# A sparse 3x3 convolution: the first 32 rows of the input are loaded by two transfers instead of one

## The chip, the core and the metric

The kernel runs on one core of one Trainium2 chip. The metric is device time in microseconds (us). Below, PE is the matrix engine, PEld its weight loads, DVE the vector engine, ACT the scalar engine, POOL the GpSimd engine and SP the engine that here only issues transfers. A core has 16 DMA engines that every transfer is spread over.

## The reference

`x` is 16 images of 64 channels of 64x64, float32. `weight` is 128x64x3x3, float32, nine tenths of it zero; the kernel treats it as dense.

```python
x_pad = np.pad(x, ((0, 0), (0, 0), (pad, pad), (pad, pad)), mode='constant')
output = np.zeros((batch, c_out, h, w), dtype=np.float32)
for b in range(batch):
    for co in range(c_out):
        for ci in range(c_in):
            for kh in range(k):
                for kw in range(k):
                    if weight[co, ci, kh, kw] != 0:
                        output[b, co] += weight[co, ci, kh, kw] * x_pad[b, ci, kh:kh+h, kw:kw+w]
```

The input is 16.8 MB and the output 33.6 MB, both float32.

## The kernel before

**Tiling.** Two images of 64 channels fill the 128 partitions, so there are eight pairs, `xs[0]` to `xs[7]`, each a bf16 tile of 128 x 64 x 64 (rows x columns). Image 0 of a pair sits in the lower 64 partitions, image 1 in the upper 64, and every product is a pair of matmuls, one on each half of the PE array (`64*128` in the profile).

**Loads.** Nearly all of the input comes in through POOL's transfer queue, which converts float32 to bf16 on the way (`load`, L68, and L63 for rows 32 to 63 of the first pair). The first 32 rows of the first pair come another way: SP loads them unconverted as float32 into `x_head` (L62), a tile of the output pool, right after the weights (L60), and DVE and ACT convert them (`cast_x`, L101): rows 0 to 8 on DVE (L123), rows 9 to 17 on ACT (L130), rows 18 to 31 on ACT (L133). POOL issues L63, then the loads of pairs 1 to 3 and of 24 rows of pair 4 at once; the remaining loads follow in `load` calls at the ends of later pairs.

**Weights.** The weights are cast to bf16, transposed on PE against an identity matrix (`transposed`, L111), and copied to `wT` as three row taps G0, G1, G2, with the differences G0-G1 and G2-G1 beside them (`difference`, L115). Around this PE runs matmuls on a zero tile that go nowhere (`keep_busy`, L86): seven before the transposes and seven after.

**Work.** Each pair is cut into four blocks of 16 rows. The first block of the first pair is `direct`: two times 8 rows, each nine taps on both images, 36 matmuls in all, copied out by ACT (L163) and DVE (L164). It needs rows 0 to 16 of the input. Every other block is `twos`: POOL adds neighbouring rows (`s`, L169), PE multiplies the sums once by G1 (6 matmuls), ACT copies the result to SBUF (`pc`, L176), and PE multiplies even and odd rows by the other taps (24 matmuls), whose results DVE adds to `pc` (L183). The second block of the first pair (rows 16 to 31) is the first `twos`; its `s` needs all rows that the second ACT conversion (L133) writes.

**Order.** The schedule is manual: each engine runs its instructions in the order in which the code issues them. On PE that is seven idle matmuls, the transposes, seven idle matmuls, the direct block, then the `twos` blocks. SP issues the weights, the head, the two stores of each pair as the pair ends (L209, half-pair stores for the last pair, L206), and after pair 1 four loads of one word each into a spare tile (L216). The transfers on SP take their completion semaphores in turn from a set of eight.

Of the kernel before, what the change touches and what calls it, by code (L numbers as in the profile page):

```python
# [27 lines left out]
def kernel(  # L28
# [6 lines left out]
    nc = tc.nc  # L35
# [2 lines left out]
    C_OUT, _, KH, KW = weight.shape  # L38
    assert (B, C_IN, H, W) == (16, 64, 64, 64) and (C_OUT, KH, KW) == (128, 3, 3)
    NP = B // 2  # L40
    HEAD = 32

    const_pool = ctx.enter_context(tc.tile_pool(name="const", bufs=1))
    x_pool = ctx.enter_context(tc.tile_pool(name="x", bufs=1))
# [10 lines left out]
    def pair(p):  # L55
        return x[2 * p : 2 * p + 2].rearrange("n i h w -> (n i) h w")
# [2 lines left out]
    w_sb = const_pool.tile([C_OUT, C_IN * KH * KW], FP32, name="w_sb")  # L59
    nc.sync.dma_start(out=w_sb, in_=weight.rearrange("o i kh kw -> o (i kh kw)"))  # L60
    x_head = o_pool.tile([128, H, W], FP32, name="o")
    nc.sync.dma_start(out=x_head[:, 0:HEAD, :], in_=pair(0)[:, 0:HEAD, :])  # L62
    nc.gpsimd.dma_start(out=xs[0][:, HEAD:H, :], in_=pair(0)[:, HEAD:H, :])  # L63
    ident = const_pool.tile([128, 128], BF16, name="ident")
    make_identity(nc, ident)

    def load(p, a=0, b=H):
        nc.gpsimd.dma_start(out=xs[p][:, a:b, :], in_=pair(p)[:, a:b, :])  # L68
# [15 lines left out]
    def keep_busy(n):  # L84
        for _ in range(n):
            nc.tensor.matmul(idle_ps, idle_rhs[:, 0:128], idle_rhs, start=True, stop=True)  # L86
# [13 lines left out]
    def cast_x(copy, a, b):  # L100
        copy(out=xs[0][:, a:b, :], in_=x_head[:, a:b, :])  # L101
# [12 lines left out]
    def difference(g, wps):  # L114
        nc.vector.tensor_tensor(out=wT[:, g], in0=wps, in1=wT[:, G1], op=SUB)  # L115
# [11 lines left out]
    ps2 = transposed(G2)  # L127
    nc.scalar.copy(out=wT[:, G2], in_=ps2)
    keep_busy(7)
    cast_x(nc.scalar.copy, 9, 18)  # L130
    difference(G01, ps0)
    difference(G21, ps2)
    cast_x(nc.scalar.copy, 18, HEAD)  # L133


    def product(terms, rows):
# [22 lines left out]
    def direct(p, o, r0, rows):  # L159
        ps = product(  # L160
            [(xs[p], G1, r0, 1), (xs[p], G0, r0 - 1, 1), (xs[p], G2, r0 + 1, 1)], rows
        )
        nc.scalar.copy(out=o[0][:, r0 : r0 + rows, :], in_=ps[0])  # L163
        nc.vector.tensor_copy(out=o[1][:, r0 : r0 + rows, :], in_=ps[1])  # L164

    def twos(p, o, r0):
        t0 = r0 // 2
        s = s_pool.tile([128, 8, W], BF16, name="s")
        nc.gpsimd.tensor_tensor(  # L169
            out=s, in0=xs[p][:, r0 : r0 + 16 : 2, :], in1=xs[p][:, r0 + 1 : r0 + 16 : 2, :], op=ADD  # L170
        )
        shared = product([(s, G1, 0, 1)], 8)
        pc = []
        for n in range(2):
            c = p_pool.tile([128, 8, W], FP32, name="pc")
            nc.scalar.copy(out=c, in_=shared[n])  # L176
            pc.append(c)
        even = [(xs[p], G21, r0 + 1, 2), (xs[p], G0, r0 - 1, 2)]
        odd = [(xs[p], G01, r0, 2), (xs[p], G2, r0 + 2, 2)]
        for first, terms in ((r0, even), (r0 + 1, odd)):  # L180
            ps = product(terms, 8)
            for n in range(2):
                nc.vector.tensor_tensor(  # L183
                    out=o[n][:, first : r0 + 16 : 2, :], in0=ps[n], in1=pc[n], op=ADD
                )

    for p in range(NP):
        o = [o_pool.tile([C_OUT, H, W], FP32, name="o") for _ in range(2)]
        last = p == NP - 1
        for blk in range(4):  # L190
            r0 = 16 * blk
            if BLOCKS[p][blk] == "T":
                twos(p, o, r0)


                if p == 1 and blk == 3:
                    load(EARLY, CUT, H)
                elif blk == 3 and p in LATER:
                    load(*LATER[p])
            else:  # L200
                for r, rows in ((r0, 8), (r0 + 8, 8)):
                    direct(p, o, r, rows)
            if last and blk % 2 == 1:
                for n in range(2):
                    rows = slice(r0 - 16, r0 + 16)
                    nc.sync.dma_start(out=out[2 * p + n][:, rows, :], in_=o[n][:, rows, :])  # L206
        if not last:
            for n in range(2):
                nc.sync.dma_start(out=out[2 * p + n], in_=o[n])  # L209
        if p == 1:  # L210

            spare = const_pool.tile([1, 4], FP32, name="spare")
            for k in range(4):
                nc.sync.dma_start(out=spare[:, k : k + 1], in_=weight[0:1, 0, 0, 0:1])  # L216


# [28 lines left out]
```

## Time and profile before

| what | value |
|---|---|
| median of 3 runs | 126.06 us (125.97 to 126.77) |
| the profiled execution: span from the first to the last instruction | 127.2 us |
| PE busy | 111.3 us (87%) |
| DVE busy | 82.4 us (65%) |
| POOL, ACT busy | 41.7 us, 38.9 us |
| moved by DMA | 42.91 MB in the queues' count, HBM read 17.07 MB, written 33.55 MB |
| mean granted PE clock | 0.955 |

The profiled execution has one time, its span: 127.2 us, 1.1 us above the median of the timed runs. Bytes in the queues are counted on the side that is written, so a converting load of 4 KB in bf16 reads 8 KB. The share of the 16 DMA engines that is busy stands beside the engines' busy times in the profile's rows of windows; it may exceed 1 in a short window, because a packet is counted where it starts.

### The profile page before, as it was taken

Reading aid. Unit: us, or ns where it says so; the run is one execution under the profiler, and the core shown is the slowest. Engines: PE = TensorE matmul, PEld = TensorE weight load, DVE = VectorE, ACT = ScalarE, POOL = GpSimd, SP = SyncE. Lnnn points to the kernel's source line nnn. Section 1 sums busy time; section 2 is a strip of 40 time slices with the busy share of each in tenths; the row PEclk is TensorE's granted clock in tenths of the full one; section 3 lists DMA queues with packets and bytes.
Section 4 is the critical chain, followed back from the end, with each engine's and each line's share of the span. In section 5 each row is a group of like instructions: output and inputs, shape, how many; then the busy total and the mean of one; then the engine's idle time right before and its main releaser. Section 6 shows DMA issues by size and latency. Waiting matters only on the chain.

```text
span 127.2 us, 2468 instructions
## 1 busy us (share of the span) xinstructions
PE 111.3 (87%) x989; PEld 57.9 (46%) x989; DVE 82.4 (65%) x135; ACT 38.9 (31%) x71; POOL 41.7 (33%) x47
## 2 busy tenths in 40 slices
PE   6939999999999999999999999999999999991000
PEld 2414455555555555555555555555555555550000
DVE  0305357787778777877787778777877787775000
ACT  4504343333333333333333333333333333330000
POOL 6405433353335333533353335333333330000000
PEclk9995999999999999999999999999999999999755
DMA  4999999659999999999999999999999999999991
GB/s 131 346 228 214 222 222 206 137 247 412 299 323 397 419 281 299 330 428 330 296 322 430 353 345 420 413 374 345 421 417 412 433 433 438 412 422 415 435 410 77
DMA packets 4339, 42.91 MB, mean 337 GB/s; under 512 B 488, under 2 KB 488, under 8 KB 1256
## 3 DMA queue, kind: packets, MB, share of 16 engines
q1 hardware_dynamic: 2888, 34.90, 66.0%
q0 software_dynamic: 1440, 7.86, 30.0%
q8 instruction: 7, 0.11, 0.3%
q14 instruction: 4, 0.03, 0.1%
HBM read 17.07 MB, written 33.55 MB: 398 GB/s over the span
## 4 chain that ended last, share of the span: by engine, by line
PE 82%; DMA 6%; DVE 1%; issue 1%; DVEq 0%; SPq 0%
PE ps L150 82%; DMA o<-in_x_dram 6%; DVE o L183 1%; DVEq L242 0%; DVE x L101 0%; SPq L60 0%; DVEq L183 0%
## 5 line engine op out<-in xcount | busy, mean ns | idle before, releaser
L150 PE MATMUL ps<-x,wT 64*128 64x504 bf16 (+3 forms) x780 | 90.5, 379 | 2.3 <-DVE x L101 2.3
L183 DVE TENSOR_TENSOR o<-ps,pc 128x512 f32<-128x512 f32 x124 | 77.8, 685 | 22.1 <-PE ps L150 19.8
L150 PEld LDWEIGHTS <-wT 64*128 64x128 bf16 x966 | 55.3, 95 | 52.0 <-issue 4.7
L169 POOL TENSOR_TENSOR s<-x 128x512 bf16<-128x512 bf16 x31 | 35.6, 1151 | 61.2 <-PE ps L150 42.7
L176 ACT COPY pc<-ps 128x512 f32<-128x512 f32 x62 | 33.3, 589 | 64.0 <-issue 61.8
L150 PE MATMUL ps<-s,wT 64*128 64x512 bf16 (+1 forms) x186 | 25.7, 377 | 0.0
L86 PE MATMUL ps<-idle_rhs 128*128 128x512 bf16 x14 | 5.5, 562 | 1.2 <-DVE idle_rhs L81 1.2
L68 POOL DMA_DIRECT2D x<-in_x_dram x9 | 5.0, 560 | 0.0
L164 DVE COPY o<-ps 128x512 f32<-128x512 f32 x2 | 1.4, 692 | 3.7 <-PE ps L150 3.7
L101 DVE CAST x<-o 128x576 bf16<-128x576 f32 x1 | 0.5, 460 | 4.6 <-DMA o<-in_x_dram 4.6
L86 PEld LDWEIGHTS <-idle_rhs 128*128 128x128 bf16 x14 | 1.8, 136 | 3.6 <-issue 2.2
L105 DVE CAST w_bf<-w_sb 128x192 bf16<-128x192 f32 (+1 forms) x4 | 1.1, 357 | 2.4 <-DMA w_sb<-in_weight_dram 2.4
L101 ACT CAST x<-o 128x576 bf16<-128x576 f32 (+1 forms) x2 | 1.5, 802 | 3.5 <-DMA o<-in_x_dram 3.5
L163 ACT COPY o<-ps 128x512 f32<-128x512 f32 x2 | 1.2, 585 | 4.1 <-PE ps L150 4.1
L105 ACT ACT_TABLE_LOAD x1 | 1.3, 1283 | 0.7 <-PEq L231 0.7
L105 ACT CAST w_bf<-w_sb 128x64 bf16<-128x64 f32 (+1 forms) x2 | 0.7, 416 | 1.6 <-DMA w_sb<-in_weight_dram 1.6
L111 PE MATMUL ps<-ident,w_bf 128*128 128x128 bf16 x9 | 1.2, 309 | 0.0
L111 PEld LDWEIGHTS <-w_bf 128*128 128x128 bf16 x9 | 0.8, 130 | 0.8 <-DVE w_bf L105 0.7
L115 DVE TENSOR_TENSOR wT<-ps,wT 128x384 bf16<-128x384 f32 x2 | 1.0, 547 | 0.0
L63 POOL DMA_DIRECT2D x<-in_x_dram x1 | 0.7, 693 | 0.8 <-POOLq L231 0.8
L81 DVE MEMSET idle_rhs<- 128x256 uint32 x1 | 0.3, 272 | 0.9 <-PEq L231 0.9
L124 ACT CAST wT<-ps 128x384 bf16<-128x384 f32 x1 | 0.5, 478 | 0.4 <-PE ps L111 0.4
(8 smaller groups left out, 1.9 us busy)
## 6 DMA issues: line engine op xcount, KB each, us to landing
out_dram<-o SPq DMA_DIRECT2D x14, 2048.0 KB, 15.1
x<-in_x_dram POOLq DMA_DIRECT2D x5, 1024.0 KB, 15.9
out_dram<-o SPq DMA_DIRECT2D x4, 1024.0 KB, 10.8
x<-in_x_dram POOLq DMA_DIRECT2D x3, 512.0 KB, 13.3
o<-in_x_dram SPq DMA_DIRECT2D x1, 1024.0 KB
x<-in_x_dram POOLq DMA_DIRECT2D x1, 640.0 KB, 15.4
x<-in_x_dram POOLq DMA_DIRECT2D x1, 384.0 KB, 21.9
w_sb<-in_weight_dram SPq DMA_DIRECT2D x1, 288.0 KB
```

The lines of the kernel that those rows point to most:

```text
L68: nc.gpsimd.dma_start(out=xs[p][:, a:b, :], in_=pair(p)[:, a:b, :])
L86: nc.tensor.matmul(idle_ps, idle_rhs[:, 0:128], idle_rhs, start=True, stop=True)
L101: copy(out=xs[0][:, a:b, :], in_=x_head[:, a:b, :])
L105: copy(out=w_bf4[:, g, a:b, :], in_=w_v[:, k : k + b - a, :])
L111: nc.tensor.matmul(wps[:, j, :], src, ident, start=True, stop=True)
L115: nc.vector.tensor_tensor(out=wT[:, g], in0=wps, in1=wT[:, G1], op=SUB)
L150: nc.tensor.matmul(ps[n][:, lo:hi, c_lo:c_hi], tap(g, kw, n), src[q, a:b:step, c_lo + kw - 1 : c_hi + kw - 1], start=(i == 0), stop=(i == ...
L163: nc.scalar.copy(out=o[0][:, r0 : r0 + rows, :], in_=ps[0])
L164: nc.vector.tensor_copy(out=o[1][:, r0 : r0 + rows, :], in_=ps[1])
L169: nc.gpsimd.tensor_tensor(out=s, in0=xs[p][:, r0 : r0 + 16 : 2, :], in1=xs[p][:, r0 + 1 : r0 + 16 : 2, :], op=ADD)
L176: nc.scalar.copy(out=c, in_=shared[n])
L183: nc.vector.tensor_tensor(out=o[n][:, first : r0 + 16 : 2, :], in0=ps[n], in1=pc[n], op=ADD)
```

## The change

The transfer of rows 0 to 31 becomes two transfers on the same queue, of rows 0 to 17 and of rows 18 to 31, issued one after the other. Both have a completion semaphore of their own, so the conversions of rows 0 to 8 (DVE) and 9 to 17 (ACT) wait for the first transfer only and the conversion of rows 18 to 31 (ACT) for the second. One of the four one-word loads after pair 1 goes, so that the number of transfers on SP is the same from there on. The order of instructions on PE, DVE, ACT and POOL is the same.

```diff
-    HEAD = 32
+    FIRST, HEAD = 18, 32
...
     x_head = o_pool.tile([128, H, W], FP32, name="o")
-    nc.sync.dma_start(out=x_head[:, 0:HEAD, :], in_=pair(0)[:, 0:HEAD, :])
+    for a, b in ((0, FIRST), (FIRST, HEAD)):
+        nc.sync.dma_start(out=x_head[:, a:b, :], in_=pair(0)[:, a:b, :])
     nc.gpsimd.dma_start(out=xs[0][:, HEAD:H, :], in_=pair(0)[:, HEAD:H, :])
...
-    cast_x(nc.scalar.copy, 9, 18)
+    cast_x(nc.scalar.copy, 9, FIRST)
     difference(G01, ps0)
     difference(G21, ps2)
-    cast_x(nc.scalar.copy, 18, HEAD)
+    cast_x(nc.scalar.copy, FIRST, HEAD)
...
             spare = const_pool.tile([1, 4], FP32, name="spare")
-            for k in range(4):
+            for k in range(3):
                 nc.sync.dma_start(out=spare[:, k : k + 1], in_=weight[0:1, 0, 0, 0:1])
```

## The prediction

> **What bounds the kernel now.** I read the chain of waits first.
>
> ```profile
> 1.18 8.12 DMA o<-in_x_dram
> 9.30 0.02 issue
> 9.33 0.47 DVE x L101
> 9.80 0.04 issue
> 9.84 103.77 PE ps L150 x954
> ```
>
> PE starts real work at 9.84, when the head has landed (9.30) and DVE has converted nine rows, and then never stops. The timeline shows what lies around that start.
>
> ```profile
> 5.15 2.35 PE L86 MATMUL ps<-idle_rhs 128*128 128x512 bf16 x7
> ...
> 9.33 0.46 DVE L101 CAST x<-o 128x576 bf16<-128x576 f32 x1 [4.61 <-DMA o<-in_x_dram]
> 9.33 1.51 ACT L101 CAST x<-o 128x576 bf16<-128x576 f32 x2 [3.46 <-DMA o<-in_x_dram]
> ...
> 9.84 5.67 PE L150 MATMUL ps<-x,wT 64*128 64x512 bf16 x36 [2.34 <-DVE x L101]
> ...
> 10.92 3.37 POOL L169 TENSOR_TENSOR s<-x 128x512 bf16<-128x512 bf16 x3 [6.31 <-ACT x L101]
> ...
> 15.33 0.83 PE L150 MATMUL ps<-s,wT 64*128 64x512 bf16 x6
> 15.98 2.77 PE L150 MATMUL ps<-x,wT 64*128 64x512 bf16 x24
> ```
>
> The idle matmuls keep PE until 7.50, so a head that is there before that gains nothing more. PE idles 2.34 us, and the direct block's 36 matmuls take 5.67 us, where 24 later ones take 2.77 (36 would take 4.15): 1.5 us go to a granted clock of 0.50 in the window 10 to 12. So the late head costs PE 2.34 + 1.5 = 3.8 us.
>
> Does the end follow PE? PE's last matmul starts at 114.5 and DVE's last add at 115.5, but the span ends at 127.2: the last 11 us are stores draining. The windows by microsecond tell the rest (the width, busy time of PE, PEld, DVE, ACT, POOL with counts, then granted clock, share of the DMA engines, GB/s).
>
> ```profile
> 23.00:24.00 1.00, 1.00 (x14) 0.49 (x11) 0.30 (x1) 0.79 (x2) 0.96 (x1) 1.00 1.02 202
> 24.00:25.00 1.00, 1.00 (x14) 0.57 (x12) 0.97 (x2) 0.00 (x0) 0.00 (x0) 1.00 0.49 92
> 25.00:26.00 1.00, 1.00 (x12) 0.55 (x10) 1.00 (x3) 0.13 (x1) 0.03 (x1) 1.00 0.05 9
> 26.00:27.00 1.00, 1.00 (x14) 0.57 (x10) 0.51 (x1) 0.94 (x2) 1.00 (x1) 1.00 0.62 262
> ```
>
> The DMA engines are full from 2 us until 124.5 except here, between the last early load and the first store (issued at 26.0). The kernel is bound by its transfers; PE's start matters only through this hole. The trace's packet records give it for each engine: fourteen idle 2.1 to 2.7 us, two only 1.2 and 1.4, because their loads end later. An earlier PE therefore gains at least 1.2 us (those two) and at most about 2.3 (the mean of the others), however early it is.
>
> **Why the head is late.** It lands when the last of 16 engines is done. By the semaphore records, fifteen engines report between 5.69 and 6.62; one reports at 9.30. On the fifteen, the eight 8192 B packets (309 ns each) run back to back and POOL's loads begin after the eighth (seventh on two of them). On the late engine POOL's first packet came in at 3.92, after one head packet, and from then on one head packet and one load packet take turns (head packets at 5.84, 6.46, 7.09, 7.71, 8.33). The same taking of turns, one for one whatever the sizes, is in steady state: at 33 to 40 us stores of 16384 B (611 ns) and loads of 5120 B (398 ns) alternate with a period of 1.0 us.
>
> So everything hangs on whether an ordinary execution has that engine. With it gone, PE would start at 7.5, the hole would close, and the span would be 127.2 minus 1.2 to 2.3, thus 124.9 to 126.0. The timed runs' median, 126.06, lies 1.1 below this span. I take that as the likelier reading (about 0.55): most timed runs have no such late engine, and the profiled one does.
>
> **The change part by part.**
>
> *Packets.* 2304 B take 93 ns and 8192 B 309, so 0.0367 ns per byte between: 4608 B take 178 and 3584 B 140. Eight of each are 1.42 + 1.12 = 2.54 us on an engine, against 8 x 0.309 = 2.47: +0.07 us of work, nothing at 122 us of it. SP's extra issue is 0.42 us (L62's own row), behind which SP has nothing until 26.0.
>
> *First transfer, ordinary engines.* Their head data starts at about 2.9 to 3.2, so the first transfer is through at 4.3 to 4.6 and lands, 0.4 later (5.30 to 5.69 in the records), at 4.7 to 5.3 if the semaphore waits one turn. DVE converts until 5.8, ACT its nine rows until 6.0, and DVE's copy to `wT` (0.55) ends by 6.4. PE is still in its idle matmuls until 7.50. Against a head that lands at 6.62 (converted by 7.1) this gains nothing: 7.50 either way.
>
> *Second transfer, ordinary engines.* Loads came in after the eighth packet of the queue, so the second transfer's eight packets probably take turns with L63's eight of 4096 B (322 ns): 8 x (0.322 + 0.140) = 3.7, from 4.6 to 8.3, plus one turn for the semaphore and the 0.4: 9.0. If they do not take turns it is 6.1. ACT's conversion (0.93, the longer of its two) ends at 9.9, POOL's `s` (1.15) at 11.1. PE wants it at 7.50 + 4.15 = 11.65. Cover: 0.5 us, and behind it the hole, 1.2 to 2.3 us, as stores would be ready at about 22.2 while loads run to 24.5. I cost it at nothing; without either cover each microsecond costs one.
>
> *The wait it adds.* ACT's conversion of rows 18 to 31 now waits for a transfer of its own; queued behind it on ACT are the copies of the direct block (L163) and every `pc`, and on POOL every `s`.
>
> *The spare load.* Its four rows stand at 39.9 to 43.3 on SP at 1.0 to 1.3 us each; the next store is issued at 51.6. One fewer: nothing. The semaphores of the first four stores shift by one place; each previous user has landed long before its reuse.
>
> The Trainium skill, "DMA: Bandwidth & Descriptors", section "Rules for kernel authors", speaks against splitting: at least 1 MiB per transfer, and the section on one transfer's anatomy gives about 2.0 us fixed for each. By an estimate from that, the second half would land 2.0 us after 6.62, at 8.6; the rows give 6.1 to 9.0, and both are early enough.
>
> *Sum:* 0 on PE's start, +0.07 on the DMA engines: 126.06 becomes **126.1**, its own range 125.5 to 126.9.
>
> **The rivals.**
>
> *Slower: the second transfer starves on the late engine.* Suppose that engine is in every run. Its first transfer then takes turns with L63: from 3.92 some six or seven packets at 0.322 + 0.178 = 0.5, through at about 7.3, landed at 8.0 (9.30 before). But now eight more packets are to take turns, and L63 is nearly used up: its successor's packets are 8192 B at 0.625 us. Two turns of 0.46 and six of 0.765 are 5.5; with semaphore turns (0.3 and 0.6) and the 0.4 it lands at about 14.0 to 14.5 instead of 9.30. Conversion 0.93 and `s` 1.15 end at 16.1 to 16.6; `s` is wanted at 15.33 today. PE has run dry by then, so another half-speed stretch (1.5, today's price) is possible. Cost 0.8 to 2.9 us, price 1.9: 128.0. It decides from the point where the second transfer lands after 13.2 (15.33 - 1.15 - 0.93), or, where PE starts at 7.5, after 9.5 plus the hole's cover. For it: the turns are in the trace. Against it: one engine of sixteen, seen once. 0.33.
>
> The skill's same page, "Latency and other measured facts", says that DMA engines 7 and 15 are usually slower in traces. The packet records here do not number the engines, so no row shows it. If the late engine is one of them, it is late in every run and this rival's 128.0 stands; by the trace alone it may be chance.
>
> *Faster: the late engine is in every run before, and the shorter first transfer gets past it.* If the first 8 packets of 178 ns are fetched before POOL's descriptors are there and the second lands by 13, PE starts at 7.5 to 8.5 at full clock, 2.8 to 3.8 us earlier; the hole caps it at 1.2 to 2.3: 123.8 to 124.9, say 124.4. For it: the wait is the head of the chain. Against it: the median lies below the span already. 0.20.
>
> *It does not do what it says:* both halves land together, since the loads stay out until sixteen packets are through. Then nothing changes; this is in the forecast's 0.47.
>
> **Numbers.** No change 0.47 (126.1), slower 0.33 (126.9 to 129.0), faster 0.20 (123.8 to 124.9). About 1%, 1.26 us, is what a measurement of this kernel can tell from no change, so the bounds are 124.8 and 127.3. The range leaves out half of the faster case and the top of the slower one: 124.3 to 128.6.
>
> **What would show it.** Right: the DVE conversion waits until about 5, PE's direct block starts at 7.5 without half clock, `s` of the second block is done before 11.7, and the DMA share has no hole at 24 to 26. The slower rival: ACT's second L101 row starts at 13 or later, PE's `ps<-s` row at 12 to 16 waits for POOL or ACT, and the clock halves again. The faster one: PE as in the first case, with runs clearly under 125. I am wrong if the timed runs of before have the late engine after all, or if taking turns hits the second transfer harder than the 0.5 us of cover and the hole can bear.

## The result

The changed kernel is slower. Its median is 128.34 us (127.09 to 130.18, 6 runs), beside 126.11 us (125.97 to 126.77) for the kernel before in the same comparison; the ratio is 1.0123, 95% interval 1.0084 to 1.0161, or 1.5 us (1.1 to 2.0). Some executions of both kernels take 1.5 us or more longer than the rest, for reasons that no trace here shows; ratios and intervals leave them out, which is why this one is below the quotient of the medians.

The profiled execution after has a span of 125.3 us and a time of 127.09: about 1.8 us lie around the span, in most runs of the study 1.7 to 2.0. So the profile that was shown of before, with its span of 127.2, was not that of an ordinary run at 126.1. An ordinary one came with the first experiment, span 124.2, and it is the one to compare with.

The chain of waits after (start, us, what):

```profile
1.64 9.75 DMA o<-in_x_dram
11.39 0.02 issue
11.41 0.95 ACT x L102
12.36 0.07 issue
12.44 1.16 POOL s L170
13.59 0.04 issue
13.63 98.28 PE ps L151 x918
```

It no longer runs through the first rows. It runs through the second transfer: landed at 11.39, converted by ACT, added by POOL, and only then PE's 918 remaining matmuls, without a stop to the end. The timeline of the same execution shows what PE did meanwhile.

```profile
5.24 1.67 PE L87 MATMUL ps<-idle_rhs 128*128 128x512 bf16 x7
...
5.88 0.46 DVE L102 CAST x<-o 128x576 bf16<-128x576 f32 x1 [0.98 <-DMA o<-in_x_dram]
...
6.84 3.98 PE L151 MATMUL ps<-x,wT 64*128 64x512 bf16 x36
...
11.41 0.94 ACT L102 CAST x<-o 128x896 bf16<-128x896 f32 x1 [4.86 <-DMA o<-in_x_dram]
...
12.44 4.48 POOL L170 TENSOR_TENSOR s<-x 128x512 bf16<-128x512 bf16 x4 [7.83 <-ACT x L102]
13.63 0.82 PE L151 MATMUL ps<-s,wT 64*128 64x512 bf16 x6 [2.81 <-POOL s L170]
```

The first transfer does what it says: landed at 5.86, and PE starts the direct block as soon as its idle matmuls end. It finishes at 10.82 and waits 2.81 us. The hole in the transfers at 24 to 26 us, of which the prediction made so much, is hardly there (last columns: granted clock, share of the DMA engines, GB/s).

```profile
23.00:24.00 1.00, 1.00 (x14) 0.55 (x11) 1.00 (x3) 0.00 (x0) 0.00 (x0) 1.00 0.87 172
24.00:25.00 1.00, 1.00 (x14) 0.54 (x12) 0.81 (x2) 0.83 (x2) 0.73 (x1) 1.00 1.04 206
25.00:26.00 1.00, 1.00 (x12) 0.53 (x10) 0.59 (x1) 0.24 (x1) 0.93 (x2) 1.00 1.26 455
```

### The profile page after: what moved, and what is told of

It is laid out like the page before. It is cut to its first block, busy times and chain, and to the rows that moved or that the text cites. A ratio compares the mean times of both kernels' runs of the same rounds, so it can differ in the third digit from the quotient of the medians.

```text
span 125.3 us, 2468 instructions
## 1 busy us (share of the span) xinstructions
PE 109.1 (87%) x989; PEld 57.1 (46%) x989; DVE 82.5 (66%) x135; ACT 38.8 (31%) x71; POOL 41.6 (33%) x47
## 4 chain that ended last, share of the span: by engine, by line
PE 78%; DMA 8%; DVE 1%; POOL 1%; ACT 1%; issue 1%; SPq 1%; DVEq 0%
PE ps L151 78%; DMA o<-in_x_dram 8%; DVE o L184 1%; POOL s L170 1%; ACT x L102 1%; DVEq L243 0%; SPq L63 0%; SPq L60 0%; DVEq L184 0%
## 5 line engine op out<-in xcount | busy, mean ns | idle before, releaser
L151 PE MATMUL ps<-x,wT 64*128 64x504 bf16 (+3 forms) x780 | 88.8, 373 | 0.0
L87 PE MATMUL ps<-idle_rhs 128*128 128x512 bf16 x14 | 4.8, 505 | 1.2 <-DVE idle_rhs L82 1.2
```

The source lines that it names most:

```text
L151: nc.tensor.matmul(ps[n][:, lo:hi, c_lo:c_hi], tap(g, kw, n), src[q, a:b:step, c_lo + kw - 1 : c_hi + kw - 1], start=(i == 0), stop=(i == ...
```

## The experiments

Each ratio is against the kernel before, run beside it on the same chip.

**One transfer, once more** (no edit).

> The kernel before once more, for its span in an ordinary execution; the profile at hand has a span of 127.2 us with one DMA engine reporting the head at 9.30. If that engine is an exception (the reading of the prediction), the profile shows the head landed by 6.7, PE's direct block at about 7.0 to 7.5, the first store issued at about 22 and a span near 124.5 to 125. If it is the rule, PE starts again at 9.8 and the span is again 127.

126.28 us, ratio 0.9985 (0.9955 to 1.0016), span 124.2. Its timeline:

```profile
5.11 2.38 PE L86 MATMUL ps<-idle_rhs 128*128 128x512 bf16 x7
...
6.76 0.46 DVE L101 CAST x<-o 128x576 bf16<-128x576 f32 x1 [2.09 <-DMA o<-in_x_dram]
...
7.42 3.98 PE L150 MATMUL ps<-x,wT 64*128 64x512 bf16 x36
...
8.36 3.37 POOL L169 TENSOR_TENSOR s<-x 128x512 bf16<-128x512 bf16 x3 [3.76 <-ACT x L101]
...
11.24 0.81 PE L150 MATMUL ps<-s,wT 64*128 64x512 bf16 x6
```

All 16 engines report the head between 5.63 and 6.74, PE goes from the idle matmuls into the direct block and from it into the second block without a wait, and the first store is issued at 21.92. The late engine at 9.30 was an exception: of the 76 timed runs of the kernel before that stand beside the experiments, 74 have spans of 124.1 to 125.6, and only two are as long as the profile of before (127.2 and 127.9). Against this run the change has PE's second block start 2.4 us later (13.63 against 11.24), although its first block starts 0.6 us earlier.

**Two transfers, POOL's loads later.**

```diff
-    nc.gpsimd.dma_start(out=xs[0][:, HEAD:H, :], in_=pair(0)[:, HEAD:H, :])
     ident = const_pool.tile([128, 128], BF16, name="ident")
     make_identity(nc, ident)
+    delay = const_pool.tile([128, 512], BF16, name="delay")
+    for _ in range(3):
+        nc.gpsimd.memset(delay, 0.0)
+    nc.gpsimd.dma_start(out=xs[0][:, HEAD:H, :], in_=pair(0)[:, HEAD:H, :])
```

> The two transfers as in the change, but POOL first builds the identity and fills a scratch tile three times, so that its loads are issued 1.5 to 2 us later. Theory of turns (the second transfer is late because its eight packets per engine take turns with POOL's loads, which are there from 4.7 us): the second transfer lands at 6 to 7 instead of 11.39, PE does not idle before its first ps<-s matmuls, and the time falls back to 125.5 to 126.5. Rival, the split itself costs (a second transfer, smaller packets, a second semaphore) whoever else loads: 127.5 to 128.5 as for the change.

126.55 us, ratio 1.0009 (0.9976 to 1.0042). The load of rows 32 to 63 is issued at 2.89 instead of 1.24, its first packet moves from 4.73 to 5.85, and the second transfer lands at 6.20 to 6.84. The timeline:

```profile
6.04 1.76 ACT L105 CAST x<-o 128x576 bf16<-128x576 f32 x2
...
7.88 1.15 POOL L173 TENSOR_TENSOR s<-x 128x512 bf16<-128x512 bf16 x1 [2.19 <-ACT x L105]
7.90 3.98 PE L154 MATMUL ps<-x,wT 64*128 64x512 bf16 x36
...
11.72 0.81 PE L154 MATMUL ps<-s,wT 64*128 64x512 bf16 x6
```

No wait before the second block, and the loss is gone. The split alone, without POOL's packets between, does not cost what the change costs.

**The cut at row 30 instead of 18.**

```diff
-    for a, b in ((0, FIRST), (FIRST, HEAD)):
+    for a, b in ((0, 30), (30, HEAD)):
```

> The cut of the two transfers at row 30 instead of 18; conversions as in the change, so rows 18 to 31 wait for both. The second transfer has 512 B per packet instead of 3584, a seventh of the bytes, but still eight packets per engine. Theory of turns: its lateness hardly shrinks (eight turns of 0.32 us or more after the first transfer, which ends at about 5.6): landed at 9 to 10.5, PE idle before ps<-s 1 to 2.5 us, 127 to 128. Rival, bytes decide (the second transfer is 448 KB behind a full queue): it lands by 7, no idle, 126.

126.49 us, ratio 1.0018 (0.9991 to 1.0044). The second transfer, a seventh of the bytes, still lands at 8.60 to 9.39, 3.1 us after the first (6.33), while the first lands no later than the undivided head. That is the lateness of turns, not of bytes. But the wait that I expected of it (1 to 2.5 us) is 0.21:

```profile
9.41 0.94 ACT L102 CAST x<-o 128x896 bf16<-128x896 f32 x1 [2.39 <-DMA o<-in_x_dram]
...
11.64 0.82 PE L151 MATMUL ps<-s,wT 64*128 64x512 bf16 x6 [0.21 <-POOL s L170]
```

Landed at 9.39, the rows are converted and added by 11.60, just 0.21 us after PE wanted them. So lateness counts from a landing of about 9.2 in this trace, near the 9.5 that the prediction gave where PE starts at 7.5.

**All four spare loads kept** (`range(4)` in the change).

> The two transfers, but all four spare loads kept, so the spare part of the change is undone. If the spare load matters for nothing, 127.1 to 129 as for the change. If the slower time came from the shift of semaphores of the first stores or from the count of transfers, it moves: the later stores each shift by one place in the set of eight, and a change of more than 1 us either way would show it.

129.05 us, ratio 1.0121 (1.0059 to 1.0184): the change's own ratio. The spare load is not the cause. In this trace fifteen engines report the second transfer by 10.35 and one at 12.11; PE waits 2.81 us again, span 126.5.

**The second transfer cut again**, rows 18 to 24 and 25 to 31, two spare loads.

```diff
-    for a, b in ((0, FIRST), (FIRST, HEAD)):
+    for a, b in ((0, FIRST), (FIRST, 25), (25, HEAD)):
```

> The second transfer cut again, rows 18 to 24 and 25 to 31: the same bytes in sixteen packets per engine instead of eight; two spare loads. Theory of turns: eight more turns, now against packets of 8192 B at 0.625 us: the last one lands at about 14 to 15 instead of 11.4, PE idles 5 to 7 us before its second block, which starts at about 17, and the time is 130 to 131.5. Rival, bytes or a fixed cost per transfer decide: 128 to 128.6.

134.37 us, ratio 1.0625 (1.0568 to 1.0682). The same bytes in twice the packets: the second part lands at 9.71, the third at 15.22, 5.5 us later, as eight turns against packets of 0.625 us ask for. That was expected at 14 to 15. The time was not (130 to 131.5):

```profile
17.53 1.46 PE L151 MATMUL ps<-s,wT 64*128 64x512 bf16 x6 [6.37 <-POOL s L170]
```

6 matmuls take 1.46 us instead of 0.82. PE had idled 6.37 us, and its granted clock is 0.50 in the windows that follow.

```profile
15.00:17.00 2.00, 0.00 (x0) 0.00 (x0) 0.00 (x0) 1.70 (x3) 0.68 (x1) 0.77 1.00 209
17.00:19.00 2.00, 1.47 (x8) 0.64 (x9) 0.00 (x0) 0.21 (x1) 2.00 (x3) 0.50 1.06 221
19.00:21.00 2.00, 2.00 (x12) 0.78 (x10) 0.00 (x0) 1.07 (x2) 1.79 (x2) 0.50 1.06 221
21.00:23.00 2.00, 2.00 (x14) 0.78 (x12) 1.29 (x2) 0.00 (x0) 0.00 (x0) 0.53 1.03 217
```

So the first store goes out at 30.83, and PE's idling costs twice: once as a wait, once at half clock. The half clock was not in what I expected.

**What a late PE costs by itself.** One transfer, PE held back by more idle matmuls ahead of the direct block; the loads are untouched.

```diff
-    keep_busy(7)
+    keep_busy(12)   # and 20, and 38
     cast_x(nc.scalar.copy, 9, 18)
```

> One transfer, 12 idle matmuls instead of 7 ahead of the direct block: PE is 5 x 0.216 = 1.1 us later, the first store is issued at about 23.0 instead of 21.9. If lateness is free as long as stores start before the early loads end (store issue before about 23.6), 126.1 to 126.6 as with 7. Rival, each microsecond of PE costs the same from the start (0.8 us for 2.8 in the run with 20): 126.6 to 126.9.

> The kernel before (one transfer), with 20 idle matmuls instead of 7 ahead of the direct block: PE is held back by 13 x 0.216 = 2.8 us, so its second block starts at about 14.0 instead of 11.24, close to the 13.63 of the changed kernel; the loads are untouched. If the late second block alone carries the cost of the change, the time rises by as much: 127.3 to 128. Rival, the cost is in the DMA engines (slower packets, one more transfer) and not in PE: 126.3 to 126.8.

> One transfer, 38 idle matmuls: PE is 6.7 us later, its second block starts at about 18, close to the 17.5 of the kernel with three transfers, the first store at about 28.7. If late stores carry the cost, one for one behind the point where the early loads end: span 129.5 to 130, time 131.5 to 132. Rival, the transfers themselves carry most of the 8 us of the three-transfer kernel: 129 or less here.

| idle matmuls | first store issued | median | ratio (95%) | span |
|---|---|---|---|---|
| 7 | 21.92 | 126.28 | 0.9985 (0.9955 to 1.0016) | 124.2 |
| 12 | 22.88 | 126.12 | 0.9984 (0.9957 to 1.0010) | 124.5 |
| 20 | 24.88 | 127.52 | 1.0062 (1.0020 to 1.0104) | 126.0 |
| 38 | 27.98 | 131.41 | 1.0388 (1.0333 to 1.0444) | 129.2 |

The first microsecond is free; from 24.88 to 27.98, 3.1 us of lateness cost 3.2 us of span. (The medians differ by 3.9, but the ten timed runs with 20 idle matmuls have spans from 124.9 to 126.2, and the traced one is among the longest.) The windows of the last run show why: here is the hole again, about as wide as the store is late.

```profile
24.00:25.00 1.00, 1.00 (x12) 0.49 (x10) 1.00 (x3) 0.32 (x1) 0.22 (x1) 1.00 0.52 98
25.00:26.00 1.00, 1.00 (x14) 0.44 (x10) 0.28 (x1) 0.76 (x2) 0.94 (x1) 1.00 0.06 12
26.00:27.00 1.00, 1.00 (x14) 0.49 (x12) 1.00 (x2) 0.00 (x0) 0.00 (x0) 1.00 0.00 0
27.00:28.00 1.00, 1.00 (x12) 0.44 (x10) 1.00 (x3) 0.16 (x1) 0.06 (x1) 1.00 0.00 0
28.00:29.00 1.00, 1.00 (x12) 0.49 (x10) 0.49 (x1) 0.92 (x2) 1.00 (x1) 1.00 0.62 262
```

In this last trace the head has a straggler again: fifteen engines report by 6.50 and one at 8.49. It costs nothing here, since PE wants the rows only at 13.49, but a late engine as such is not as rare as the spans of before suggest.

**The change once more** (no edit).

> The changed kernel once more, for a second trace and more times. Theory: its times spread because the second transfer lands when the slowest of 16 engines has taken its turns, which differs from run to run (11.39 and 12.11 in the two traces at hand): landed anywhere from 10.5 to 14, the first store issued at 24 to 27, the span 124.9 plus what the first store is later than 24, so 125.2 to 128; ratio to one transfer 1.008 to 1.015. Rival, a fixed cost: landing within 0.3 us of 11.4 and runs within 0.5 us of each other.

127.49 us, ratio 1.0102 (1.0043 to 1.0161), span 125.2. The second transfer lands at 10.38 this time, a little before the 10.5 to 14 that was expected; PE waits 1.88 us, and the first store is issued at 23.30, before the expected 24 to 27.

```profile
12.63 0.83 PE L151 MATMUL ps<-s,wT 64*128 64x512 bf16 x6 [1.88 <-POOL s L170]
```

The landing does differ from run to run (10.38, 11.39, and 12.11 with four spare loads), and so the landing is no fixed delay. But the span (125.2) is as long as with the first store at 24.31 (125.3), so the first store alone does not set it.

**Rows 18 to 31 through POOL's queue**, four spare loads.

```diff
-    for a, b in ((0, FIRST), (FIRST, HEAD)):
-        nc.sync.dma_start(out=x_head[:, a:b, :], in_=pair(0)[:, a:b, :])
+    nc.sync.dma_start(out=x_head[:, 0:FIRST, :], in_=pair(0)[:, 0:FIRST, :])
+    nc.gpsimd.dma_start(out=xs[0][:, FIRST:HEAD, :], in_=pair(0)[:, FIRST:HEAD, :])
...
-    cast_x(nc.scalar.copy, FIRST, HEAD)
```

> Rows 18 to 31 come through POOL's queue, converted on the way and ahead of its other loads, instead of through SP; ACT's second conversion is gone, four spare loads. Theory of turns: with both in one queue nothing takes turns with the second transfer but the end of the first; it lands by 7 to 7.5, s of the second block is done by 9, no idle PE, 126.0 to 126.6. Rival, a second transfer costs by itself: 127 or more.

126.52 us, ratio 1.0015 (0.9981 to 1.0049). It lands by 6.67 on fifteen engines and at 7.82 on the last; `s` is done at 9.1, the second block starts at 10.42, 0.8 us before that of one transfer. Two transfers for the same rows without the turns, and no loss or gain that the interval can tell from nothing.

**What the split could have brought.** Two transfers, POOL's loads later, and 2 idle matmuls instead of 7.

> The two transfers with POOL's loads issued later, as in the run before, and 2 idle matmuls instead of 7 ahead of the direct block: PE starts at about 6.7 to 7.0 instead of 7.9. This is what the change could have brought with its second transfer in time. If the transfers bound the kernel, about 126.3 as with one transfer (a gain under 0.4 us). Rival, PE's start counts one for one: 125.4 to 125.7.

126.67 us, ratio 1.0022 (0.9999 to 1.0045). PE starts at 6.29, the second block at 10.09, the first store at 20.76, all over a microsecond ahead of one transfer, and the time is if anything longer. The transfers bound this kernel, and PE's start is worth nothing once it is early enough.

**The control**: one transfer, POOL's loads later.

> One transfer, with POOL's loads issued later as in the run with two transfers: the control for that run. The head lands at 6.5 to 7, nothing takes turns with it. If the split gains nothing once its second half is in time, the time is the same as there (126.2 to 126.8). If the split with late loads hid a gain behind the cost of the later loads, this one is slower than it by 0.5 us or more.

126.83 us, ratio 1.0031 (0.9992 to 1.0070), with an interval that overlaps that of two transfers (1.0009). So no gain of the split is seen behind the cost of the later loads; one of a few tenths of a microsecond could not be seen this way.

None of the versions beats the kernel before.

## Why the prediction was right, and where it was not

The measured median lies in the range, but the likeliest case did not come: I put "no change" at 0.47 and "slower" at 0.33, and it is slower, by 1.0 to 1.2% in two comparisons. That the range holds it is partly luck: the range reaches that far for the sake of the slower rival, whose condition, a late engine in every run, was not met. Step by step:

**The late engine was an exception: right for one as late as 9.30.** An ordinary run has PE at 7.4, no half clock and no hole, as the first experiment shows; a lesser straggler (8.49) stands in one of the four other traces with one transfer and early loads. The comparison that led there was wrong by its size: the time was set against the span as if they were one measure, while about 1.8 us lie around the span. The profiled execution stood not 1.1 but some 3 us above an ordinary one (127.2 against 124.2). By the same rows the prediction's bound, that an earlier PE gains "at most about 2.3", was too low: 3.0 us lie between the two spans. It counted the hole alone, but the packets also took longer in the profile of before, 122.92 us per engine in all against 122.26.

**The first transfer gains nothing: right.** It lands at 5.86 (4.7 to 5.3 predicted) and PE is then still in its idle matmuls. Even with PE 1.1 us earlier than with one transfer nothing is gained (2 idle matmuls, 126.67).

**The second transfer on ordinary engines: the step that failed.** The mechanism is the one written down, one packet of each queue in turn, and the sizes were wrong. The estimate was 9.0; fourteen engines report between 9.46 and 10.24 and the last two at 10.96 and 11.39. Two terms of it were too small. The 4608 B packets, priced at 178 ns from the line through two sizes, took 246 on average, so the first 3584 B row starts at 5.48 instead of 4.6. (They took 246 with POOL's loads held back too, so the loads are not the reason; what is stays open.) And I took all engines to run out of 4096 B load packets only after the eight turns: an engine on which the turns begin within the first transfer has used some of them up, and meets the 0.625 us packets behind (the first load row starts at 4.73, the last 4608 B row at 5.39; the first 0.625 us packet at 8.19, the last 3584 B row at 10.31). That was worked out for a late engine only, as a rival; in a milder form it is in all three traces of this split, and a transfer lands with its slowest engine. The kernel with three transfers shows the same arithmetic in the large (15.22).

Two rules can be held against these rows. The Trainium skill, "DMA: Bandwidth & Descriptors", section "Queues, rings and completion order", has an engine drain a whole packet of typically 9 to 17 descriptors from one queue before it turns to the next. Here the turns are single descriptors once they begin: the most frequent distance between the starts of two 3584 B rows is 0.45 us, a little less than their 0.153 plus the 0.322 of one load row, and over all engines rows of both kinds start at about the same rate. By the page's rule the eight rows would have gone in one turn; the measurement decides. The fixed 2.0 us per transfer of the same page's anatomy section, which the page gives for transfers that GpSimd issues and the prediction weighed for these of SP, is not seen either: with POOL's loads out of the way the second transfer lands 1.1 us after the first (5.73 and 6.84).

**The cover of 0.5 us: too large here.** PE's idle matmuls took 1.67 us in the run after, 2.38 with one transfer, so the direct block ended at 10.82, not 11.65. Thus `s`, expected at 11.1 and wanted at 11.65, came at 13.59 and was wanted at 10.82: 2.81 us of idle PE.

**The hole as second cover, 1.2 to 2.3 us: nearer to 1.** A first store that is 1.0 us later costs nothing, one that is 3.0 us later costs 0.8 us by the ratio (0.6% of 126.3). By that line the change's first stores (23.30 and 24.31) would cost about 0.2 and 0.6 us, and the two comparisons give 1.3 and 1.5. But by the span of the traced execution, the one whose first store is known, 3.0 us cost 1.8 (126.0 against 124.2), so the line is too flat for a store as late as 24.31.

**The rest: longer packets.** The packet records say where the traced execution of the change, 1.1 us longer than that of one transfer (125.3 and 124.2), spends it. There is almost no hole; the packets of one DMA engine took 123.43 us in all against 122.26, 1.17 us more, and the DMA engines are full to the end. Beyond the fastest twentieth of their own size and queue, packets that started in the first 10 us took 1.16 us per engine against 0.66, and those that started from 24 to 45 us, where the first stores go out, 1.11 against 0.45. The second part, 0.7 us, belongs to the late store: the run with 20 idle matmuls, whose loads are untouched, has 1.19 there. The first, 0.5 us where the prediction put 0.07, comes with the two transfers, but no run isolates it: two transfers with later loads have 1.00 in the first 10 us, and their span is only 0.2 us longer (124.4), less than the ratio's interval can show. The second trace of the change has 1.24 in the first part, 0.54 in the other and 122.99 in all: 0.7 of its 1.0 us of extra span. Why the first packets take longer, and that last 0.3 us, stay open.

**The rivals.** "Slower" came true in mechanism, at some three quarters of its price (1.3 to 1.5 us for 1.9) and without its condition. (Its upper cost, 2.9, is 2.8 by its own terms: 16.6 less 15.33, plus 1.5.) "Faster" is ruled out by the first experiment, which has no engine as late as 9.30, and by the run with 2 idle matmuls, where an early PE gains nothing. The spare load is nothing, as predicted.

## What to carry to other kernels

A transfer cut in two on one queue puts its second half at the mercy of whatever another queue has ready: count its packets per engine, not its bytes, multiply by the other queue's packet time, and look at the slowest engine. Before pricing a head start, find out whether the end follows it at all; here 1 us earlier or later at the start moved nothing, because the stores keep the DMA engines full until the end. And a single profiled execution may be an exception: compare its time, not its span, with the median before building on what is odd in it.

## What the runs showed of the hardware that was not expected

- Idle time alone does not tell whether PE's clock halves. In the profile of before 2.34 us of idling were followed by a granted clock of 0.50 in the window 10 to 12; after, 2.81 us (10.82 to 13.63) were not, and the clock stayed at 1.00 until PE was done. After 6.37 us (three transfers) it was 0.50 from about 16.1 to 22.9, worked out from the means of 0.77 and 0.53 in the windows at the two ends.
- The seven idle matmuls before the direct block took 1.67 to 1.93 us in some runs and 2.35 to 2.54 in others, with nothing changed on PE: with one transfer they start 0.43 us apart until 6.4 us and 0.22 us apart after, in the run after 0.22 us apart from the first.
- When the two first stores go out behind the loads, their packets get slower: 16384 B packets that started between 30 and 40 us took 618 ns on average with the first store at 21.92, and 696 and 688 with it at 24.88 and 27.98. So lateness costs more than the hole itself: per engine, all packets took 122.93 us in both of the latter, 122.26 in the first.
